# Layer 1's residual and softmax sums turned in 32x32 squares and carried through DRAM by GpSimd

## The chip, the cores and the metric

The kernel runs on one core of a Trainium2 chip. A core has a matrix engine (TensorE, PE in the views, with its weight loads as PEld), a vector engine (VectorE, DVE), a scalar engine (ScalarE, ACT), GpSimd (POOL) and a queue processor (SyncE, SP), which here issues all transfers. The engines run their own instruction streams in order and wait for each other by semaphores. The metric is the device time of one execution in microseconds; the time before is 1944.4 us, the median of three runs (1944.25 to 1944.41).

## The reference

Two layers of a decoder trunk on 1024 tokens of width 1024, all in float32. Layer 0 mixes tokens with gated linear attention in chunks, layer 1 with sparse attention: an indexer scores the keys of every query, the 256 best are kept, and 16 heads of 128 attend to these. Each layer then adds a residual, normalises, and adds a gated projection.

```python
def dsa_mixer(x, ...):                       # layer 1, shortened
    h = x @ w_in                             # q, k, v, z and the indexer's qi, ki, wi
    ...
    logits = jnp.where(valid, q_b . k_sel * ATTN_SCALE, -jnp.inf)
    probs = jax.nn.softmax(logits, axis=-1)
    o = probs . v_sel
    return (o * jax.nn.silu(z)) @ w_out

for i in range(DEPTH):
    y = gla_mixer(x, ...) if i % 3 == 0 else dsa_mixer(x, ...)
    x = layer_norm(ALPHA * x + y, ln_g[i], ln_b[i])          # the residual: ALPHA * x
    x = x + (p[i] @ ple_w[i]) * jax.nn.sigmoid(x @ ple_gate_w[i])
```

## The kernel before

Tokens are handled in two halves of 512, first both halves of layer 0, then both of layer 1. Activations lie feature-major: a tile [128, 512] has 128 features on the partitions and 512 tokens along them, and the 1024 features are 8 tiles k. For precision every matmul operand is split into a high part and the rest (`split`: ACT copies to the rounding type fp32r, DVE subtracts), and each product is three matmuls, high x high, high x low, low x high (`fm_block`: 24 matmuls of 128x512 for one block of 128 output features, into one of three PSUM banks `pb`). Weights are split on the way in during layer 0 and, by `split_ahead`, once more stored split in DRAM, from where later uses load them (`whi`, `wlo`).

The program is written by a planner in Python, `Flow`. It counts a planned time as it issues PE work (0.213 us for a 512-wide matmul, 0.109 for a transpose) and keeps a heap of functions with planned times (`fl.at`, `after`, `chain`); after every step of the PE stream it issues those that are due, so the place of an instruction in its engine's stream follows from its planned time. `feed_by` does the same for a generator at a fixed gap. A function may refuse and is tried again 0.3 us later.

In layer 1, a half is a row of slots, one for each head h from -1 to 15. In a slot PE runs the units of later or earlier work (q and z blocks for heads ahead, output products of heads done) while the attention of head h (PE: probabilities x V, tiles `ph`, `PT`, `o`) and the scores of head h + 1 (`A`: PE scores into `S`, DVE adds the mask and takes the extreme, ACT takes the exponential with its sum, DVE turns the result in 32x32 squares, SP stores it to DRAM and loads it back, which completes the transposition) are spread between them. `parts` then splits the loaded probabilities (ACT `ph`, DVE `PT`), `pv` multiplies them. The sum of each query's exponentials, `sm` [128 queries, 4], must become a row along the free axis: `inverse` takes the reciprocal, PE transposes it to [4, 128], ACT copies it out of PSUM, SP stores it as `row` and, in `to_all`, loads it to all partitions as `inv`; DVE multiplies z by it.

The layer's output is made token-major (`accumulate` adds a PSUM bank to `y[:, t, ...]`, 128 tokens by 512 features), since the norm runs over features. Its residual is layer 0's result x2, which lies feature-major in DRAM (`x2s`): `residual` loads each of the 8 tiles again, PE turns it with four transposes into a `pb` bank, and ACT writes it to y with the factor ALPHA. This happens at the ends of the slots of heads 0 to 3. `norm_steps` collects statistics and applies them in place; `tail` turns y back with 32 transposes and runs eight gate blocks (`("t", layer, b)`), whose operands `gx` come from splits. In half 0 of layer 1 a top-k search for the second half's queries runs in the background on DVE and ACT (`bg`).

Of the kernel before, what the change touches and what calls it, by code (L numbers as in the profile page):

```python
# [277 lines left out]
def trunk_kernel(ctx, tc, x_tok, x_T, p_T, pos, freq, g_q, g_k, g_v, g_z, g_a, g_a2, g_ba, g_gn, g_o,  # L278
# [178 lines left out]

    def narrow(w, n, t):
# [170 lines left out]
    def core_steps(u):  # L629
# [175 lines left out]
    def accumulate(parts, U, y, ch, rs=None, norm=None, ahead=1):  # L805
# [5 lines left out]
        for t, b in order:  # L811
# [11 lines left out]
            ys = y[:, t, ch * 512:ch * 512 + 512]  # L823
# [30 lines left out]
    def norm_steps(y, np_, eps, on_act=()):  # L854
# [6 lines left out]
        def norm(t, ch):  # L861
# [7 lines left out]
            dve.bn_stats(st8[:, t, ch], y[:, t, ch * 512:ch * 512 + 512])  # L869
# [5 lines left out]
            def apply():  # L875
                if t in on_act:
                    act.activation(y[:, t], y[:, t], AF.Identity, scale=rstd[:, t:t + 1], bias=mv[:, t, 1:2])
                else:
                    dve.tensor_scalar(y[:, t], y[:, t], mv[:, t, 0:1], rstd[:, t:t + 1],
                                      op0=OP.subtract, op1=OP.mult)  # L880
                f_done[t] = True
# [23 lines left out]
    def tail(layer, Pt, y, y_done, final, tp, xps, x_alloc, tmp, ple=(), first=None, shared=False, split_last=False):  # L905
# [10 lines left out]
        def xpose(k):  # L916
            fl.need(lambda: all(y_done))
            ps = xps()
            for t in range(4):
                fl.transpose(ps[:, t * 128:t * 128 + 128], y[:, t, k * 128:k * 128 + 128], ident)  # L920
# [20 lines left out]
        for b in range(NK):  # L941
            def ev(ps, ts=slice(0, HT), b=b):
# [3 lines left out]
                def gated():  # L946
# [3 lines left out]
                      (1.5, lambda: final(b, x1, ts) if cut else final(b, x1)))  # L950
            cut = split_last and b == NK - 1
            yield from fm_block(("t", layer, b), X, ev, *([(slice(0, 256), slice(256, HT))] if cut else []))
# [50 lines left out]
    def small_head(half, X, f32t, alloc, qalloc, tmp, spsum, kih, kil, res):  # L1003
# [30 lines left out]
        yield from fm_block(("ki",), X, ev_ki)  # L1034
        for b in range(4):
            def ev_qi(ps, b=b):
# [11 lines left out]
            yield from fm_block(("qi", b), X, ev_qi)  # L1048

    def small_kv(half, X, f32t, alloc, tmp, spsum, kh, kl, vh, vl, res):  # L1050
# [14 lines left out]
        def ev_v(ps):  # L1065
# [14 lines left out]
            chain((0, lambda: act.activation(vf, ps, AF.Copy, scale=0.5)), (1.2, turn))  # L1080
# [144 lines left out]
    def start_half(half):  # L1225
# [15 lines left out]
        def feed():  # L1241
            if half == 0:
                load(0, 1)
                W.loads(W.ns + 1)
                load(1, 1)
                W.loads(W.ns + 2)
                for k in range(2, NK, 2):
                    load(k, 2)
# [28 lines left out]
    for half in range(NH):  # L1277
        hs = slice(half * HT, half * HT + HT)
        if half == 0:
# [8 lines left out]
            feed_by(feeder, 0.0, 0.0)  # L1288
# [5 lines left out]
        y = X.y  # L1294

        def load_y(y=y, half=half):
# [50 lines left out]
        norm, y_done = norm_steps(y, lp, EPS / ALPHA ** 2)  # L1347
# [120 lines left out]
    def x2_tiles(half):  # L1468

        def load(k):  # L1470
            st = xp.tile([128, HT], F32, tag="xst", name="xst", bufs=2)
            nc.sync.dma_start(st, x2s[k, :, half * HT:(half + 1) * HT])
            return st
        st = load(0)
        for k in range(NK):
            nxt = load(k + 1) if k + 1 < NK else None
            yield
            yield k, st
            st = nxt

    def feed_x2(X, half):
        for i in range(2):
            nc.sync.dma_start(tabs[i], rope_s[i, 0:32, half * HT:(half + 1) * HT])
        for got in x2_tiles(half):
            if got:
                X.put(*got)
            yield

    def residual(st, y, half, ks, start, end):

        tiles = {}

        def load(k):
            tiles[k] = xp.tile([128, HT], F32, tag="xst", name="xst", bufs=2)
            nc.sync.dma_start(tiles[k], x2s[k, :, half * HT:(half + 1) * HT])

        def by_token(k):
            ps = pbank()
            for t in range(4):
# [253 lines left out]
    for half in range(NH):  # L1753
# [13 lines left out]
        for h, units in enumerate(plan, -1):  # L1767
# [36 lines left out]
            if h == 0:  # L1804
                y = xp.tile([128, 4, D], F32, tag="y", name="y")
# [87 lines left out]
```

## Time and profile before

| | |
|---|---|
| median of 3 runs | 1944.4 us |
| the profiled execution, its own time | 1945.97 us |
| its span, first to last instruction | 1944.2 us |
| granted TensorE clock | 1.000 |
| PE busy | 1924.8 us, 8912 matmuls and transposes |
| DVE, ACT, POOL busy | 1481.8, 1014.5, 55.2 us |
| bytes moved | 480.50 MB, all the kernel's own from one queue |

The page gives, for each engine, the busy time and its share of the span. Matmuls overlap in the pipeline, so that the durations of single ones add up to more than the busy time; what one costs PE is seen from start to start. The views named below are: the groups by line (an operation's count, busy time and mean duration, then the idle time before it and what ended that), the waits (who waited for whom: us in total, times, the longest), the timelines of an engine (start, duration), and the table of stretches.

### The profile page before, as it was taken

How to read it: one execution, taken by the hardware profiler on the slowest of the kernel's cores; microseconds unless marked ns; L12 is line 12 of the kernel's file. 1: busy time of each engine (PE TensorE's matmuls, PEld its weight loads, DVE VectorE, ACT ScalarE, POOL GpSimd, SP SyncE). 2: the span in 40 equal slices, each digit the busy share in tenths (PEclk: the TensorE clock that was granted, in tenths of full speed). 3: DMA queues.
4: the chain of work that ended last, by engine and by line, in shares of the span. 5: the costliest groups of instructions: out<-in, count | busy, mean ns of one | idle time of the engine just before them, and what ended most of it. 6: DMA issues, size and time to landing. Idle time of an engine off the chain costs nothing.

```text
span 1944.2 us, 26708 instructions
## 1 busy us (share of the span) xinstructions
PE 1924.8 (99%) x8912; PEld 1596.4 (82%) x8912; DVE 1481.8 (76%) x3039; ACT 1014.5 (52%) x1930; POOL 55.2 (3%) x115
## 2 busy tenths in 40 slices
PE   9999999999999999999999999999999999999999
PEld 7888888888788888888888888888878888888877
DVE  5777666696778888888859987778797887777873
ACT  5564636445564646464635676766443554434432
POOL 0000000010000000000100000000000000000000
PEclk9999999999999999999999999999999999999999
DMA  4567776767668777677686588877867998888873
GB/s 155 201 222 229 221 226 214 227 210 268 227 196 266 226 212 233 220 226 218 207 304 222 194 308 292 276 271 259 317 221 236 365 323 300 299 297 300 294 260 144
DMA packets 195818, 480.50 MB, mean 247 GB/s; under 512 B 22496, under 2 KB 39008, under 8 KB 189536
## 3 DMA queue, kind: packets, MB, share of 16 engines
q1 hardware_dynamic: 195680, 478.79, 73.8%
q8 instruction: 70, 1.15, 0.2%
q14 instruction: 68, 0.56, 0.1%
HBM read 338.98 MB, written 139.72 MB: 246 GB/s over the span
## 4 chain that ended last, share of the span: by engine, by line
PE 88%; DVE 4%; ACT 4%; DMA 2%; issue 1%; SPq 0%; POOL 0%; ACTq 0%; DVEq 0%
PE pb L58 66%; PE o L58 8%; PE U L58 6%; PE S L58 6%; DMA wlo<-wls 1%; PE tr L58 1%; ACT x L926 1%; DVE wlo L191 0%; DVE bn L869 0%; DMA xst<-x2s 0%; DMA y<-in_x_T 0%; DVE y L827 0%; PE pb L62 0%; PE ix L58 0%; DMA row<-uf 0%
## 5 line engine op out<-in xcount | busy, mean ns | idle before, releaser
L58 PE MATMUL pb<-x,whi 128*128 128x512 f32 x2272 | 705.4, 391 | 1.1 <-DVE x L411 1.0
L58 PEld LDWEIGHTS pb<-x,whi 128*128 128x128 f32 x2272 | 418.2, 188 | 81.2 <-DVE x L411 2.2
L58 PE MATMUL pb<-x,wlo 128*128 128x512 f32 x1136 | 442.8, 390 | 0.0
L58 PE MATMUL pb<-whi,u 128*128 128x512 f32 x1024 | 339.9, 392 | 1.5 <-ACT u L419 0.8
L58 PEld LDWEIGHTS pb<-x,wlo 128*128 128x128 f32 x1136 | 213.2, 188 | 45.7 <-DVE wlo L191 0.4
L58 PEld LDWEIGHTS pb<-whi,u 128*128 128x128 f32 x1024 | 192.1, 188 | 41.4 <-ACT u L419 1.2
L58 PE MATMUL pb<-wlo,u 128*128 128x512 f32 x512 | 199.8, 390 | 0.5 <-DMA wlo<-wls 0.5
L191 DVE TENSOR_TENSOR wlo<-wst,whi 128x512 fp32r<-128x512 f32 x232 | 154.3, 684 | 37.5 <-ACT whi L189 37.4
L189 ACT ACTIVATE whi<-wst 128x512 fp32r<-128x512 f32 x232 | 136.5, 622 | 69.4 <-DMA wst<-in_g_k 23.5
L1553 ACT ACTIVATE sq<-P,mx 128x128 f32<-128x128 f32 (+7 forms) x128 | 98.9, 773 | 88.2 <-DVE mx L1546 67.5
L58 PE MATMUL S<-kT,q 128*128 128x512 f32 (+2 forms) x576 | 122.4, 342 | 0.0
L1599 ACT ACTIVATE ph<-PT 128x512 fp32r<-128x512 f32 (+2 forms) x160 | 86.6, 559 | 65.6 <-PE o L58 46.3
L58 PEld LDWEIGHTS S<-kT,q 128*128 128x128 f32 x576 | 100.8, 188 | 18.1 <-DVE mx L1546 0.7
L58 PEld LDWEIGHTS pb<-wlo,u 128*128 128x128 f32 x512 | 96.2, 188 | 19.3 <-DMA wlo<-wls 1.3
L1597 DVE TENSOR_TENSOR PT<-PT,ph 128x512 fp32r<-128x512 f32 (+2 forms) x160 | 93.3, 594 | 21.1 <-ACT ph L1599 20.7
L1180 ACT ACTIVATE tk<-sc,tki 128x768 f16<-128x768 f32 (+2 forms) x90 | 92.8, 1031 | 18.3 <-DVE tki L1189 16.1
L1559 DVE STREAM_TRANSPOSE sq<-sq 128x128 f32<-128x128 f32 (+7 forms) x128 | 97.6, 768 | 3.2 <-ACT sq L1553 3.0
L237 DVE TENSOR_TENSOR pst<-pst,phi 128x512 fp32r<-128x512 f32 x130 | 88.7, 683 | 7.5 <-ACT phi L233 7.4
L736 ACT ACTIVATE junk<-o 128x512 bf16<-128x512 f32 x32 | 19.1, 597 | 142.1 <-DVE ot L731 109.8
L58 PE MATMUL o<-ph,vT 128*128 128x512 f32 (+2 forms) x320 | 92.4, 370 | 0.2 <-ACT ph L1599 0.2
L58 PE MATMUL pb<-whi,x 128*128 128x512 f32 x256 | 85.2, 391 | 0.7 <-ACT whi L189 0.7
L58 PE MATMUL U<-whi,x 128*128 128x512 f32 x256 | 84.5, 389 | 0.0
(324 smaller groups left out, 3325.0 us busy)
## 6 DMA issues: line engine op xcount, KB each, us to landing
whi<-whs SPq DMA_DIRECT2D x128, 512.0 KB
wlo<-wls SPq DMA_DIRECT2D x128, 512.0 KB
sqd<-sq SPq DMA_DIRECT2D x192, 256.0 KB
PT<-sqd SPq DMA_DIRECT2D x48, 1024.0 KB
whs<-phi SPq DMA_DIRECT2D x130, 256.0 KB
wls<-pst SPq DMA_DIRECT2D x130, 256.0 KB
wst<-in_g_z SPq DMA_DIRECT2D x32, 512.0 KB
wst<-in_g_o SPq DMA_DIRECT2D x32, 512.0 KB
```

What stands on the lines that cost most here:

```text
L58: self.pe.matmul(out, lhsT, rhs, start=start, stop=stop)
L189: self.nc.scalar.activation(hi[:, c], st[:, c], AF.Copy, scale=1.0 if gain is None else gain)
L191: self.nc.vector.tensor_sub(lo[:, c], st[:, c], hi[:, c].bitcast(F32))
L237: self.nc.vector.tensor_sub(st, st.bitcast(F32), hi.bitcast(F32))
L736: act.activation(junk, ps, AF.Square, accum_out=u["ss"][:, c:c + 1])
L926: act.activation(X1[k], ps, AF.Identity, scale=g, bias=b)
L1180: act.activation(junk()[:, :n], scs[j], AF.Sign, bias=cand[:, j:j + 1].bitcast(F32), accum_out=cnt[:, j:j + 1])
L1553: act.activation(to, rows, AF.Exp, scale=-1.0, bias=mx, accum_out=sm[:, t:t + 1])
L1559: dve.transpose(x, x)
L1597: dve.tensor_sub(lo, lo.bitcast(F32), hi.bitcast(F32))
L1599: chain((0, lambda: act.activation(hi, lo.bitcast(F32), AF.Copy)), (0.8, second))
```

## The change

In layer 1 the residual is no longer loaded again and turned by PE. The tile that the operands of a half were split from (`yt`: 8 feature-major tiles of x2) stays in place. For each k, `turn` lets DVE transpose the 32x32 squares of `y[:, k]` into an `xst` tile; `away` has GpSimd store it to DRAM in four DMAs of 32 partitions (tile `rd`); `back` has GpSimd load it over `y[:, k]`, now with tokens on the partitions. The eight blocks are planned 7.0 apart in half 0 and 10.5 apart in half 1. y so lies as `[p, k, a, t, i]`, features in runs of 32, and is reached through a function `y(t, a, n)`. The factor ALPHA is left out of the residual and its inverse goes into V's scale, with the norm's epsilon divided accordingly. The norm writes its result to x tiles (`to_rows`) and the tail reads it there. The next half's x2 is loaded after the norm, into the y tile, instead of through `xst` tiles.

The softmax sums become a row by squares as well: GpSimd clears a [128, 32] tile, DVE writes the reciprocals to 4 columns of it and transposes its squares, and GpSimd stores four pieces of 4 x 32. `inverse` is planned 8.5 (half 0) or 12 (half 1) after a slot's start; before, it was 3 ahead of the slot's end.

Three smaller edits go with it: `fm_two` runs two blocks together, the first k of both and then the last, for the first two gate blocks of each tail and for the indexer's ki and first qi; s3 of layer 0 ripens 2.2 after its operand's split, not 1.6; at the start x is fed with a gap of 1.3 planned us and two of its tiles are loaded ahead of the third weight.

```diff
+    def fm_two(keys, X, evacs, cut):
+        parts = [W.take(key) for key in keys]
+        banks = [pbank() for _ in keys]
+        for ks in (range(cut), range(cut, NK)):
+            for (hi, lo), ps, evac in zip(parts, banks, evacs):
+                for k in ks:
+                    xh, xl = X[k]
+                    at = slice(k * 128, k * 128 + 128)
+                    for i, (l, r) in enumerate(((hi, xh), (hi, xl), (lo, xh)), 3 * k):
+                        mm(ps, l[:, at], r, i == 0, i == 3 * NK - 1)
...
-                fl.ripe(st["At", c] + 1.6)
+                fl.ripe(st["At", c] + 2.2)
...
-                dve.tensor_add(ys, ps, ys)
+                dve.tensor_add(ys, ps.rearrange("p (x i) -> p x i", i=32), ys)
...
+                for there, row in to(t):
+                    if t in on_act:
+                        act.activation(there, row, AF.Identity, scale=rstd[:, t:t + 1], bias=mv[:, t, 1:2])
+                    else:
+                        dve.tensor_scalar(there, row, mv[:, t, 0:1], rstd[:, t:t + 1],
...
+        yield from fm_two([("t", layer, b) for b in range(2)], X, [gate(b, False) for b in range(2)], 4)
...
+        yield from fm_two([("ki",), ("qi", 0)], X, [ev_ki, query(0)], 5)
...
-            chain((0, lambda: act.activation(vf, ps, AF.Copy, scale=0.5)), (1.2, turn))
+            chain((0, lambda: act.activation(vf, ps, AF.Copy, scale=0.5 / ALPHA)), (1.2, turn))
...
-            feed_by(feeder, 0.0, 0.0)
+            feed_by(feeder, 0.0, 1.3)
...
+    def feed_x2(X, y_done, new_y):
...
+        while not all(y_done):
+            yield
+        y = new_y()
+        for k in range(NK + 3):
+            if k < NK:
+                nc.sync.dma_start(y[:, k], x2s[k, :, HT:2 * HT])
+            if k > 2:
+                X.put(k - 3, y[:, k - 3])
+            yield
...
-        def by_token(k):
-            ps = pbank()
-            for t in range(4):
-                fl.transpose(ps[:, t * 128:t * 128 + 128], tiles[k][:, t * 128:t * 128 + 128], ident)
-            act.activation(y[:, :, k * 128:k * 128 + 128], ps.rearrange("p (t c) -> p t c", c=128), AF.Copy,
-                           scale=ALPHA)
...
+        def turn(k):
+            sq = xp.tile([128, HT], F32, tag="xst", name="xst", bufs=2)
+            dve.transpose(sq.rearrange("p (m b i) -> p b m i", m=4, b=4), y[:, k])
+            after(1.0, lambda: away(k, sq))
+
+        def away(k, sq):
+            rd = dp.tile([4, 32, 4, 128], F32, tag="rd", name="rd", bufs=4)
+            for a in range(4):
+                pool.dma_start(rd[:, :, a].rearrange("m r x -> r m x"),
+                               sq[32 * a:32 * a + 32].rearrange("p (m x) -> p m x", m=4))
+            def back():
+                pool.dma_start(y[:, k], rd.rearrange("m r a x -> (m r) (a x)"))
+                st["y"] = st.get("y", 0) + 1
+            after(3.0, back)
+
         for k in range(NK):
+            fl.at(start + gap * k, lambda k=k: turn(k))
...
-            dve.reciprocal(st["sm", h], st["sm", h])
-            after(1.5, turn)
-        def turn():
-            ps = spsum()
-            fl.transpose(ps[0:4, 0:128], st["sm", h], ident)
-            inv = tmp1()[0:4, 0:128]
+            sums = l1.tile([128, 32], F32, tag="bn", name="sums")
+            pool.memset(sums, 0.0)
+            dve.reciprocal(sums[:, 0:4], st["sm", h])
+            dve.transpose(sums, sums)
             row = st["row", h] = dp.tile([4, 128], F32, tag="row", name="row", bufs=2)
             def out():
-                act.activation(inv, ps[0:4, 0:128], AF.Copy)
-                nc.sync.dma_start(row, inv)
+                for a in range(4):
+                    pool.dma_start(row[:, 32 * a:32 * a + 32], sums[32 * a:32 * a + 4])
...
-                fl.at(start + dur - 3.0, scale[0])
+                fl.at(start + (12.0 if half else 8.5), scale[0])
...
+                residual(st, yt, *((start + 5.0, 10.5) if half else (start + 33.0, 7.0)))
```

Three places show how instructions move. First PE, at the end of head 0's slot in half 0 of layer 1 (`pb<-x` is a q or z block, `o<-ph` and `o<-PT` are probabilities x V, `pb<-ident,xst` the residual's transposes, `S<-ident,sm` that of the sums), before:

```order
L62 MATMUL pb<-ident,xst 128x128 x4
L58 MATMUL o<-ph,vT_9843 128x512
L58 MATMUL o<-ph,vT_9844 128x512
L58 MATMUL o<-PT,vT_9843 128x512
L58 MATMUL pb<-x,whi 128x512 x2
L58 MATMUL pb<-x,wlo 128x512
L62 MATMUL pb<-ident,xst 128x128 x4
L58 MATMUL o<-ph,vT_9843 128x4x96
L58 MATMUL o<-ph,vT_9844 128x4x96
L58 MATMUL o<-PT,vT_9843 128x4x96
L62 MATMUL S<-ident,sm 4x128
```

and with the change:

```order
L58 MATMUL o<-ph,vT_9843 128x512
L58 MATMUL o<-ph,vT_9844 128x512
L58 MATMUL o<-PT,vT_9843 128x512
L58 MATMUL pb<-x,whi 128x512 x2
L58 MATMUL pb<-x,wlo 128x512
L58 MATMUL o<-ph,vT_9843 128x4x96
L58 MATMUL o<-ph,vT_9844 128x4x96
L58 MATMUL o<-PT,vT_9843 128x4x96
```

The transposes are gone and the products of the head stand in the same order.

Second GpSimd in the same slots, with the change (before, nothing stands there: the memset of `sq` ahead of the slots is followed by the norm's steps after them):

```order
L1629 MEMSET sums 128x32
L1636 DMA row<-sums 4x32 x4
L1521 DMA rd<-xst 32x4x128 x4
L1525 DMA y<-rd 128x512
L1521 DMA rd<-xst 32x4x128 x4
L1525 DMA y<-rd 128x512
L1629 MEMSET sums 128x32
L1636 DMA row<-sums 4x32 x4
```

Two blocks of the residual stand between the sums of one head and of the next, and each memset of `sums` comes behind a read-back.

Third DVE, in half 0 in head 0's slot, before (`PT` is the split of a part of the probabilities, `rt` and `qf` belong to a q block, `z<-z,inv` uses the sums of the head before):

```order
L1597 TENSOR_TENSOR PT<-PT,ph 128x4x96
L1159 TENSOR_SCALAR tkf<-tkf 128x1
L1597 TENSOR_TENSOR PT<-PT,ph 128x4x64
L1159 TENSOR_SCALAR tkf<-tkf 128x1
L999 TENSOR_TENSOR qf<-rt 32x512
L1605 RECIPROCAL sm<-sm 128x4
L1647 TENSOR_TENSOR z<-z,inv 128x512
```

and with the change:

```order
L1620 TENSOR_TENSOR PT<-PT,ph 128x4x96
L1186 TENSOR_SCALAR tkf<-tkf 128x1
L1630 RECIPROCAL sums<-sm 128x4
L1631 STREAM_TRANSPOSE sums<-sums 128x32
L1515 STREAM_TRANSPOSE xst<-y 128x4x4x32
L1620 TENSOR_TENSOR PT<-PT,ph 128x4x64
L1186 TENSOR_SCALAR tkf<-tkf 128x1
L1023 TENSOR_TENSOR qf<-rt 32x512
L1666 TENSOR_TENSOR z<-z,inv 128x512
```

The reciprocal, which now waits for the memset, and the two transposes stand ahead of a split of the probabilities.

More of the change, by code (lines that the diff above doesn't have):

```diff
@@ L822, in accumulate @@
                 continue
-            ys = y[:, t, ch * 512:ch * 512 + 512]
+            ys = y(t, ch * 512, 512)
             if rs is not None:
@@ L940, in tail, with gate, ev @@
             yield
-        for b in range(NK):
-            def ev(ps, ts=slice(0, HT), b=b):
+        def gate(b, cut):
+            def ev(ps, ts=slice(0, HT)):
                 sg = tmp()[:, ts]
@@ L950, in ev @@
                       (1.5, lambda: final(b, x1, ts) if cut else final(b, x1)))
+            return ev
+        yield from fm_two([("t", layer, b) for b in range(2)], X, [gate(b, False) for b in range(2)], 4)
+        for b in range(2, NK):
             cut = split_last and b == NK - 1
-            yield from fm_block(("t", layer, b), X, ev, *([(slice(0, 256), slice(256, HT))] if cut else []))
+            yield from fm_block(("t", layer, b), X, gate(b, cut),
+                                *([(slice(0, 256), slice(256, HT))] if cut else []))
     def rope_tables():
@@ L1032, in weights, with query, ev_qi @@
             res["w"] = wt
-        yield from fm_block(("ki",), X, ev_ki)
-        for b in range(4):
-            def ev_qi(ps, b=b):
+        def query(b):
+            def ev_qi(ps):
                 qf = f32t()
@@ L1047, in ev_qi @@
                 rope(qf, ci, si, swap_i, tmp, stack)
-            yield from fm_block(("qi", b), X, ev_qi)
+            return ev_qi
+        yield from fm_two([("ki",), ("qi", 0)], X, [ev_ki, query(0)], 5)
+        for b in range(1, 4):
+            yield from fm_block(("qi", b), X, query(b))
     def small_kv(half, X, f32t, alloc, tmp, spsum, kh, kl, vh, vl, res):
@@ L1245, in feed @@
                 load(1, 1)
+                load(2, 2)
                 W.loads(W.ns + 2)
-                for k in range(2, NK, 2):
-                    load(k, 2)
+                load(4, 2)
+                load(6, 2)
                 nc.sync.dma_start(ba, g_ba)
@@ L1466, in dz_phase @@
         yield from fm_block(("dz", h), X, ev)
[L1468 to L1474, printed above, removed]
-        for k in range(NK):
[L1476 to L1495, printed above, removed]
-        def by_token(k):
-            ps = pbank()
-            for t in range(4):
-                fl.transpose(ps[:, t * 128:t * 128 + 128], tiles[k][:, t * 128:t * 128 + 128], ident)
-            act.activation(y[:, :, k * 128:k * 128 + 128], ps.rearrange("p (t c) -> p t c", c=128), AF.Copy,
-                           scale=ALPHA)
-            st["y"] = k + 1
-        for i, k in enumerate(ks):
-            fl.at(start + 0.6 * i, lambda k=k: load(k))
-            fl.at(end - 3.6 + 1.6 * i, lambda k=k: by_token(k))
+    def feed_x2(X, y_done, new_y):
+        for i in range(2):
+            nc.sync.dma_start(tabs[i], rope_s[i, 0:32, HT:2 * HT])
+        while not all(y_done):
+            yield
+        y = new_y()
[4 more added lines that the diff above has]
+                X.put(k - 3, y[:, k - 3])
+            yield
```

50 lines of the change are left out of this document (31 added, 19 removed).

## The prediction

> **What bounds the kernel now.** I read the page first: the busy line, then its DMA queue.
>
> ```profile
> span 1944.2 us, 26708 instructions
> PE 1924.8 (99%) x8912; PEld 1596.4 (82%) x8912; DVE 1481.8 (76%) x3039; ACT 1014.5 (52%) x1930; POOL 55.2 (3%) x115
> q1 hardware_dynamic: 195680, 478.79, 73.8%
> ```
>
> PE is busy for all but 19.4 us of the span. One queue carries the kernel's own transfers, so no DMA of POOL's stands in this trace. The table of stretches, taken over three slots of layer 1's half 0 (where the first residual lies), shows how much room the others have (columns: stretch, its length, then busy time and count of PE, PEld, DVE, ACT, POOL, the granted clock, the DMA share, GB/s):
>
> ```profile
> 1118.00:1133.00 15.00, 14.82 (x74) 12.03 (x73) 12.85 (x34) 9.65 (x23) 0.00 (x0) 1.00 0.92 344
> 1133.00:1148.00 15.00, 15.00 (x77) 12.65 (x76) 12.51 (x34) 12.64 (x29) 0.00 (x0) 1.00 0.83 289
> 1148.00:1163.00 15.00, 14.14 (x72) 11.66 (x70) 13.05 (x37) 12.94 (x30) 0.00 (x0) 1.00 0.83 293
> ```
>
> PE sets the pace, DVE has 2.0 to 2.5 us free in 15, POOL does nothing. So PE instructions taken away count in full, if nothing else comes late.
>
> **What is removed.** The PE timeline at the first residual, where one group of four transposes and one transpose of softmax sums stand between matmuls:
>
> ```profile
> 1113.92 0.39 PE L58 MATMUL pb<-x,wlo 128*128 128x512 f32 x1
> 1114.15 0.60 PE L62 MATMUL pb<-ident,xst 128*128 128x128 f32 x4
> 1114.50 0.72 PE L58 MATMUL o<-ph,vT 128*128 128x512 f32 x2
> ...
> 1116.95 0.27 PE L62 MATMUL S<-ident,sm 128*4 128x128 f32 x1
> 1116.98 0.70 PE L58 MATMUL pb<-x,whi 128*128 128x512 f32 x2
> ```
>
> The durations overlap, so I cost from start to start: 1114.50 - 1114.15 = 0.35 us for four transposes and 0.03 for the sums. The 0.27 shown is pipeline length, not PE time. The counts, and what the evacuations cost ACT, come from the groups by line:
>
> ```profile
> L62 PE MATMUL pb<-ident,xst 128*128 128x128 f32 x64 | 9.6, 273 | 1.0 <-DMA xst<-x2s 1.0
> L62 PE MATMUL S<-ident,sm 128*4 128x128 f32 x32 | 8.7, 271 | 0.0
> L1501 ACT ACTIVATE y<-pb 128x512 f32<-128x512 f32 x16 | 9.5, 595 | 9.5 <-PE pb L62 9.0
> L1616 ACT ACTIVATE uf<-S 4x128 f32<-4x128 f32 x32 | 8.2, 255 | 21.1 <-PE S L62 21.0
> ```
>
> A: 64/4 = 16 groups x 0.35 = 5.6 us of PE. B: 32 x 0.03 = 1.0. C: the one wait of 1.0 us for `xst<-x2s`, since the tile turned is now already in SBUF. ACT loses 9.5 + 8.2 = 17.7 us, which is not on the path.
>
> **The smaller edits** aim at PE's own waits:
>
> ```profile
> PE pb L58 <- DVE wlo L191: 1.3, 3, 0.8
> PE pb L58 <- DVE gx L411: 0.8, 2, 0.6
> PE o L58 <- DVE Al L411: 0.7, 1, 0.7
> ```
>
> D: `fm_two` takes the first half of two blocks before the last operands are wanted, 12 matmuls later (12 x 0.227 = 2.7 us, three matmuls taking 0.68 in the timeline), against a longest wait of 0.6; and s3 ripens 0.6 later against 0.7. I take both waits in full: 1.5 (bounds 0 and 1.5). E: the start's waits of 1.3 are for low halves of weights that DVE reaches behind splits of x; with x fed every 1.3 planned us they alternate. I take 1.0 (bounds -0.7, if x then comes late, and 1.3). Gains: 5.6 + 1.0 + 1.0 + 1.5 + 1.0 = 10.1 us.
>
> **What is added.** DVE gets 16 transposes of 128x512 and 32 small transposes; the nearest rows:
>
> ```profile
> L731 DVE STREAM_TRANSPOSE ot<-o 128x512 f32<-128x512 f32 x29 | 20.8, 716 | 22.4 <-PE o L58 22.2
> L1605 DVE RECIPROCAL sm<-sm 128x4 f32<-128x4 f32 x32 | 5.4, 170 | 0.0
> ```
>
> A slot of half 0 gains 2 x 0.72 + 0.17 = 1.6 us of DVE work, under the 2.0 to 2.5 free, with little to spare: G = 0.5 us on PE for the lot (bounds 0 and 2.8: if only half of the 2 us lies where it is wanted, 0.6 to 0.7 in each of four slots). The normalised rows now go to x tiles, in two instructions of 512 where one of 1024 stood; four ple blocks of 6 matmuls (5.4 us) stand ahead of the first transpose that reads them: H = 0.2 (bounds 0 and 0.8). The next half's x2 loads move behind the norm, with the tail's 192 gate matmuls (43.6 us) over them, and cost nothing; uncovered, eight loads at one feed step of 2.3 each are 18 us. The wide add into y and the statistics keep their 512 elements, and the factor for the residual moves into the scale of an evacuation that is there anyway. SP loses 16 loads and 32 stores from its queue, which I count at nothing.
>
> **POOL's DMAs are the unknown.** Each block is four writes `rd<-xst` and one read `y<-rd`, each head four writes `row<-sums`. The nearest thing is the same pattern from SP in layer 0 (the view of tile od: shortest, median and longest issue in ns), and, in SP's timeline, how soon a stored row can be read on:
>
> ```profile
> L750 SPq DMA_DIRECT2D od<-ot x116: 303/434/1762, 87.2 to 917.9; - x116
> ```
>
> ```profile
> 1268.59 0.26 SPq L1617 DMA_DIRECT2D row<-uf  x1
> ...
> 1270.81 0.38 SPq L1625 DMA_DIRECT2D inv<-row  x1
> ```
>
> Let c be POOL's time for one DMA: 0.434 us if it is like SP's median, 1.762 if like SP's longest. The landing is 1270.81 - 1268.59 - 0.26 = 1.96 us. The read waits on POOL for its writes, and what queues behind it there is the next head's row and, above all, the memset of `sums`, for which DVE's reciprocal waits; behind the reciprocal on DVE stand the PT splits that PE multiplies next. How little lead these have, in the timelines of DVE and of PE:
>
> ```profile
> 1130.65 0.69 DVE L1597 TENSOR_TENSOR PT<-PT,ph 128x512 fp32r<-128x512 f32 x1 [0.74 <-ACT ph L1599]
> ...
> 1132.20 0.56 DVE L1597 TENSOR_TENSOR PT<-PT,ph 128x384 fp32r<-128x384 f32 x1
> ```
>
> ```profile
> 1131.40 0.50 PE L58 MATMUL o<-PT,vT 128*128 128x512 f32 x1
> 1133.22 0.34 PE L58 MATMUL o<-PT,vT 128*128 128x384 f32 x1
> ...
> 1147.20 0.40 PE L58 MATMUL o<-PT,vT 128*128 128x512 f32 x1
> ```
>
> Leads of 0.06 us (1130.65 + 0.69 to 1131.40) and 0.46. So a late POOL is a late DVE and nearly as late a PE. A slot is 1147.20 - 1131.40 = 15.8, less what A and B take out of it, 0.73: 15.1. Blocks stand 7.0 planned us apart, 7.46 real (0.227 us for a matmul planned at 0.213), two in a slot. POOL then needs 2 x (5c + 1.96) + 4c + 0.3 = 14c + 4.2, which fits while c is under 0.78. I take c = 0.7, a fifth of the way from SP's median of 116 to its single longest, the median being the row it is nearest to: 14.0 of 15.1, no lasting lateness. Still a read-back ends 5 x 0.7 + 1.96 = 5.5 us after its first write and is planned 3.2 after, so a memset close behind waits up to 2.3. Seven heads have one there; with 0 to 4 us between the two, the mean wait is 2.3 x 2.3 / 2 / 4 = 0.66, and after the leads PE sees some 0.3: F = 2.0 us (bounds 0, and 7 x 2.3 = 16 before any lasting lateness). Half 1, with 10.5 us between blocks, has room.
>
> [...]
>
> The sum: -10.1 + 2.0 + 0.5 + 0.2 = -7.4 us. The span goes from 1944.2 to 1936.8; the profiled execution's own time of 1945.97 lies 1.8 above its span, the median of the runs, 1944.4, only 0.2. **Forecast: 1937.0 us.**
>
> **Rivals.**
> 1. POOL cannot keep up in half 0. At c = 1.1, midway between the bounds, it needs 19.6 of 15.1, is 4.5 later after each slot, 18 after four, and PE waits it out at the reciprocals: -10.1 + 0.7 + 18 = +8.6, 1953.0. It decides from 14c + 4.2 = 15.1 + 9.4/4, c = 0.95. For it: POOL issues in order and waits for landings there at a DMA share of 0.83 to 0.92. Against it: SP's 434 ns for the same pattern.
> 2. Half 0 is paced by the softmax chain, not PE: at 1130.65 DVE had waited 0.74 for ACT's ph, and PE's next product waited for both. Then half 0's part is lost (8 x 0.35 + 16 x 0.03 = 3.3) and C with it: -3.1, 1941.3. Against it: ACT loses work ahead of that ph, and the second of the three stretches has PE busy throughout.
> 3. DVE holds POOL up. A DMA of POOL's that has to wait for the DVE instruction under way, a 0.72 us transpose or a PT split, has c near 0.7 + 0.7/2 = 1.05: POOL needs 18.9, 3.8 short, 15.2 over four slots, 1950.2. [...]
>
> **How the numbers follow.** Forecast 0.70, rival 1 0.14, rival 2 0.10, rival 3 0.06. The forecast's own range runs from 1931 (F, G and H at nothing, -10.1, and 3 us of the 19.4 idle gone with SP's shorter queue) to 1941. The whole goes up to 1947, where c is just under 1.0, leaving most of rivals 1 and 3 outside. This kernel's runs tell 0.2%, 3.9 us, from no change. Faster: nearly all of the forecast and a little of the rivals with c under 0.9, 0.69. Same: the forecast's edge, rival 2: 0.13. Slower: rivals 1 and 3 past 1948.3: 0.18.
>
> **What would show it.** Right: no `pb<-ident,xst` and `S<-ident,sm`, PE's busy time some 6 us lower, POOL's DMA rows near 0.7 us, little DVE waiting for POOL at the reciprocal, PE's gx and Al waits gone. Wrong: DVE idle at the reciprocal for microseconds (rivals 1 and 3: there the POOL rows are long, in 3 only beside DVE work), PE waiting for PT or ph in half 0 with POOL on time (rival 2), inv late for the z product, or new waits of PE in the first 50 us.

## The result, and the profile after

The changed kernel takes 1964.9 us (median of four runs, 1962.8 to 1975.5) where the kernel before, on the same chip, takes 1944.4: a ratio of 1.0111, interval 1.0089 to 1.0133. By the ratio it is slower by 21.6 us (20.5 by the medians) where 7.4 less had been forecast. The profiled execution is the longest of the four, so its waits are somewhat longer than the median's; prices below come from ratios of times, and the rows show places. A ratio's last digit, 0.0001, is 0.2 us.

From the page of the changed kernel, engines and the software DMA queue (which is POOL's: packets, MB, share of the time of 16 engines):

```profile
PE 1929.7 (98%) x8816; PEld 1597.9 (81%) x8816; DVE 1497.7 (76%) x3091; ACT 999.5 (51%) x1886; POOL 169.6 (9%) x355
...
q0 software_dynamic: 7424, 8.47, 1.4%
```

PE has the 96 fewer matmuls of the change (8912 before), yet more busy time (1924.8 before): part of it ran at a lower clock (granted 0.992 over the run, 1.000 before). The view of waits of the same kernel, for PE, DVE and POOL (us in total, times, longest):

```profile
PE o L58 <- DVE PT L1620: 23.4, 19, 5.8
PE S L58 <- DVE q L411: 3.0, 2, 2.5
PE o L58 <- ACT ph L1622: 2.8, 4, 1.6
```

```profile
DVE sums L1630 <- POOL sums L1629: 12.4, 6, 5.6
```

```profile
POOL sums L1629 <- DMA row<-sums: 71.9, 22, 5.7
...
POOL y L1525 <- DMA rd<-xst: 38.7, 7, 8.5
```

These are the rows that the prediction named as the sign of POOL being late. PE's waits for gx and Al are gone, and those for `wlo` in the start fell from 1.3 to 1.1. The view of tile rd gives POOL's own time for a DMA (ns, shortest, median, longest) and its time to landing:

```profile
L1521 POOL DMA_DIRECT2D rd<-xst x64: 548/551/683, 1097.3 to 1585.9; - x64
...
DMA to landing us min/median/max: 2.0/5.6/8.3
```

POOL is quicker at issuing than I had taken (0.55 us, not 0.7), and the landing is far longer (5.6 us, not 1.96). The timeline of one stall (start and length in us; in brackets the idle time before and what ended it):

```profile
1130.41 2.28 POOL L1521 DMA_DIRECT2D rd<-xst  x4
...
1137.22 0.57 POOL L1525 DMA_DIRECT2D y<-rd  x1 [4.53 <-DMA rd<-xst]
1137.78 0.14 POOL L1629 MEMSET sums<- 128x32 f32 x1
1137.95 0.18 DVE L1630 RECIPROCAL sums<-sm 128x4 f32<-128x4 f32 x1 [5.62 <-POOL sums L1629]
...
1138.30 0.65 DVE L1620 TENSOR_TENSOR PT<-PT,ph 128x512 fp32r<-128x512 f32 x1
...
1139.01 0.80 PE L58 MATMUL o<-PT,vT 128*128 128x512 f32 x1 [5.07 <-DVE PT L1620]
...
1139.60 1.06 PE L58 MATMUL pb<-x,whi 128*128 128x512 f32 x2
```

It reads downward as a chain: POOL's writes, their landing, the read-back, the memset behind it, DVE's reciprocal, the split of PT behind that, and PE. In the last row two matmuls take 1.06 us where they took 0.62 before the stall. The view by windows shows why, in its column PEclk, third from the end (before it busy time with instructions, PE's first, after it DMA share and GB/s). Its rows are three of the six stretches in which the clock was low; the last line adds up all six:

```profile
1122.27:1125.68 3.41, 3.41 (x12) 2.93 (x11) 3.00 (x10) 1.18 (x5) 0.00 (x0) 0.50 0.94 328
1135.92:1142.75 6.83, 3.74 (x10) 3.19 (x11) 4.17 (x12) 0.00 (x0) 4.47 (x9) 0.50 0.97 291
1173.47:1183.71 10.24, 5.92 (x16) 4.96 (x17) 2.37 (x6) 2.69 (x5) 2.79 (x6) 0.50 1.01 330
...
sum 30.74, PE 23.34 PEld 19.22 DVE 17.51 ACT 8.12 POOL 11.80; mean PE 3.89 PEld 3.20 DVE 2.92 ACT 1.35 POOL 1.97
```

With stalls of 5.1 us (from 1133.9) and 5.8 us (from 1172.0) PE was granted half its clock for 6.8 and 10.2 us. These stretches begin 2.0 and 1.5 us after the stall does, so that part of them passes while PE still waits; what they cost is half of the time in which PE had work, 3.74 and 5.92 us. In all six PE had work for 23.3 us, which is 11.7 us more than at full clock. The kernel before had no such stretch between the start and the end (granted clock 1.000).

### The profile page after: what moved, and what is told of

The parts are those of the page before. It is cut to its first block, busy times and chain, and to the rows that moved or that the text cites. A ratio compares the mean times of both kernels' runs of the same rounds, so it can differ in the third digit from the quotient of the medians.

```text
span 1973.8 us, 26916 instructions
## 1 busy us (share of the span) xinstructions
PE 1929.7 (98%) x8816; PEld 1597.9 (81%) x8816; DVE 1497.7 (76%) x3091; ACT 999.5 (51%) x1886; POOL 169.6 (9%) x355
## 4 chain that ended last, share of the span: by engine, by line
PE 83%; DVE 7%; DMA 5%; ACT 2%; issue 1%; POOL 1%; SPq 1%; DVEq 0%; POOLq 0%; ACTq 0%
PE pb L58 63%; PE o L58 7%; PE U L58 6%; PE S L58 5%; DMA rd<-xst 2%; DMA PT<-sqd 1%; DVE sq L1582 1%; PE tr L58 1%; DVE PT L1620 1%; ACT tk L1207 1%; SPq L1595 0%; DMA sqd<-sq 0%; DMA wst<-in_g_v 0%; DVE P L1569 0%; DVE tk L1230 0%
## 5 line engine op out<-in xcount | busy, mean ns | idle before, releaser
L58 PEld LDWEIGHTS pb<-x,whi 128*128 128x128 f32 x2272 | 422.6, 189 | 79.9 <-DVE x L411 1.8
L58 PEld LDWEIGHTS S<-kT,q 128*128 128x128 f32 x576 | 101.9, 191 | 23.3 <-DVE q L411 3.5
L1636 POOL DMA_DIRECT2D row<-sums x128 | 66.2, 523 | 459.7 <-DVE sums L1631 440.8
L58 PE MATMUL o<-PT,vT 128*128 128x512 f32 (+3 forms) x224 | 74.3, 355 | 23.5 <-DVE PT L1620 23.4
```

What stands on the lines that cost most here:

```text
L58: self.pe.matmul(out, lhsT, rhs, start=start, stop=stop)
L1636: pool.dma_start(row[:, 32 * a:32 * a + 32], sums[32 * a:32 * a + 4])
```

## The experiments

The theories, by the letters of the expectations: **P**, POOL's wait for landings holds DVE at the memset, DVE holds PE, and half clock follows. **C**, the added bytes crowd the DMA engines. **D**, **S** and **V**, DVE's added work or the sums' path. **W** and **Q**, PE's removed work is worth its time, or it is not, because operands set the pace. **O**, the order of matmuls. **H**, half clock after stalls.

### Taking POOL's wait away

The memset on DVE:

```
-            pool.memset(sums, 0.0)
+            dve.memset(sums, 0.0)
```

> The memset of sums is moved from POOL to DVE, so that DVE's reciprocal no longer waits for POOL; POOL still sits on each read-back until its writes have landed. Theory P (a late POOL holds DVE at the memset, DVE holds PE at PT, and PE then runs some microseconds at half clock): the four waits of 0.65 to 5.62 us of DVE for POOL in half 0 go (11.3 us), and with them PE's waits for PT there and most of the half-clock stretches of 3.4, 6.8 and 10.2 us (each costs PE half its length, 10.2 us in all): 1965 - 11 - 10 = 1944, at best 1940, at worst 1950. Theory C (the loss is the DMA engines' contention, which POOL's transfers add to): nothing of this depends on who clears sums, so 1963 to 1966. Theory D (DVE has become too full in half 0): DVE gets 32 memsets more, 1965 to 1968.

Measured 1960.6 us, 1.0083 (1.0065 to 1.0100). Only a quarter of the gain that P expected came. POOL stayed late, and DVE now met that lateness elsewhere; its waits between 1090 and 1210 us:

```profile
DVE sums L1629 <- DMA row<-sums: 3.0, 2, 1.6
DVE xst L1515 <- DMA rd<-xst: 2.7, 2, 1.4
```

The memset must wait until the row store that POOL issued late has read the tile, and the next block's transpose until POOL's writes have read theirs. A dependence through a buffer took the place of the one through the instruction.

The read-back later:

```
-            after(3.0, back)
+            after(9.0, back)
```

> The read-back of a residual block is planned 9.0 after its writes in place of 3.0; the memset stays on POOL. The writes took 2.0 to 8.3 us to land, median 5.6, so most read-backs should find their data there. Theory P: POOL's waits for rd<-xst (38.7 us before) fall under 10, DVE's waits for POOL sums from 12.4 to under 3, and the time to 1941 to 1950, much like the kernel with the memset on DVE. Theory C: the same bytes move at the same share, so 1963 to 1966; if the transfers only come into the way of others later, it could be 1970. Theory D: 1965 unchanged.

Measured 1955.6 us, 1.0050 (1.0034 to 1.0067): 12 us less than the change, and DVE's wait for POOL at the reciprocal is gone from the waits. P had expected more, 1941 to 1950, and POOL's waits for the writes' landings fell from 38.7 to 19.9 us, not under 10. Both edits together:

> Both edits together, memset on DVE and the read-back planned 9.0 after the writes. Theory P: no more than about 2 us better than the better of the two alone, since either takes away the same wait: 1939 to 1946. Theory C: 1963 to 1966. What is left above the 1937 of the forecast would be half 1's waits of PE for PT (8.8 us), where DVE had waited only 1.1 us for POOL: by P and C together some 1943 to 1947.

Measured 1955.0 us, 1.0049 (1.0034 to 1.0064), no better than the later read-back alone. P is shown and priced: the wait for landings in front of the memset costs 1.0111 - 1.0049 = 0.0062, **12 us**, the half clock behind its stalls included. It is not the whole, as P's 1939 to 1946 had it: 9.5 us above the kernel before are left.

### Whose landing it is

The four writes and the read-back of a block on SP in place of POOL:

```
-                pool.dma_start(rd[:, :, a]...
+                nc.sync.dma_start(rd[:, :, a]...
-                pool.dma_start(y[:, k], ...
+                nc.sync.dma_start(y[:, k], ...
-            after(3.0, back)
+            after(6.0, back)
```

> The residual's writes and read-backs are issued by SP in place of POOL, the read-back planned 6.0 after the writes; row stores stay with POOL and sums is still cleared there. It tells whether the late landing belongs to POOL's queue or to the load on the DMA engines. If to the queue, rd<-xst lands in about 2.8 us as SP's od<-ot does, in place of 5.6; if to the load, again in 4.5 to 6. Theory P: POOL has only row stores left, DVE's wait for POOL sums goes (under 1 us), and the time falls to 1940 to 1950, unless SP, waiting in its turn for a landing, delays sqd stores and PT loads: then PE waits for ph and PT in SP's name, and 1950 to 1965. Theory C: 1960 to 1966.

Measured 1958.4 us, 1.0067 (1.0052 to 1.0082). The view of tile rd:

```profile
L1521 SPq DMA_DIRECT2D rd<-xst x64: 303/447/1907, 1097.0 to 1576.5; - x64
...
DMA to landing us min/median/max: 1.7/5.6/9.0
```

The same median, 5.6 us, from the other queue: of the expectation's two alternatives it is the load, not POOL's queue. The DMA share here was 0.76 to 0.99 between 1100 and 1200 us; in the changed kernel SP's stores of the same 64 KB in layer 0 (`od<-ot`) landed in 2.8 us, at a mean share of 0.70 (87 to 918 us). SP could then not issue sqd stores while it waited (in half 1 ACT's `sq` waited 20.7 us behind `rd<-xst`), and PE waited for ph instead (4.2 us in half 1, longest 3.3).

### The change taken apart

The residual alone (sums as before the change), the sums alone, the small edits alone, and small edits with sums; each is a part of the diff shown above.

> The change without its softmax sums: the residual and the small edits as changed, the sums turned by PE, copied by ACT, stored by SP, as before the change. POOL's read-back keeps its early place, but nothing of DVE waits for POOL any more. Theory P (POOL at the memset) by what the three kernels before showed: worth about 10 us, so 1955, less what the sums cost DVE, plus 1 for their transposes on PE: 1953 to 1957. Theory C (the residual's way through DRAM, writes and reads of 4 MB each in place of reads of 4 MB, crowds sqd and PT while the DMA engines are busy at 0.9 and over): the rest of the loss stays whole, 1953 to 1957, with PE's waits for PT in half 1 at 6 us or more. Theory S (the rest comes from the sums' path, DVE's and the rows'): it goes, 1940 to 1946.

Measured 1954.0 us, 1.0044 (1.0029 to 1.0059), as P and C had it; S, by which it would have been 1940 to 1946, falls. POOL's read-back is early there, no memset stands behind it, and the time is that of the later read-back.

> The kernel before with the softmax sums alone done the new way (memset, reciprocal and small transpose, POOL's row stores), the residual still loaded and turned by PE. Theories P and C: POOL has only row stores of 0.5 KB, waits for their landing before the memset but for no read-back; DVE waits for POOL under 2 us; 1943 to 1946. Theory S: the loss that e3 still has, 10 us and over, stands here: 1952 to 1958. My forecast had 1.0 us of gain for it: 1943.5.

Measured 1943.5 us, 0.9991 (0.9982 to 1.0000), which is the forecast's 1.0 us of gain within the interval.

> The kernel before with the three small edits alone: two blocks side by side before the last operands, s3 ripe 0.6 later, and x fed every 1.3 in the start with its load order. My forecast counted 1.5 + 1.0 = 2.5 us for them: 1941.9. In the changed kernel PE's waits for gx (0.8) and Al (0.7) are gone and those for wlo fell only from 1.3 to 1.1, which gives 1.7: 1942.7. If their places were covered anyway: 1944.4.

Measured 1940.5 us, 0.9977 (0.9968 to 0.9987): 4.5 us of gain, more than the 2.5 forecast.

> The kernel before with the small edits and the softmax sums in squares, the residual loaded and turned by PE as before the change: the change less its residual. The two measured alone at 0.9977 and 0.9991 of the kernel before; if they add, 0.9968, 1939 against 1945. If the two get in each other's way (both use DVE in half 0), 1941 to 1944. This is the candidate that could beat both kernels, and the base of the next two runs.

Measured 1940.0 us, 0.9972 (0.9961 to 0.9982). Their gains add, and this kernel beats both. So the loss comes in with the residual: from 0.9972 to 1.0049 it costs 15 us even with POOL's waits out, although it takes 64 transposes off PE. The next runs take this 15 apart, on the kernel of 1940.0 as base.

On the kernel with both edits (1955.0) the transfers of half 1 were also moved ahead:

```
-                residual(st, yt, *((start + 5.0, 10.5) if half ...
+                residual(st, yt, *((start + 1.0, 4.5) if half ...
```

> The changed kernel with memset on DVE and the late read-back (measured 1955.0), and half 1's residual blocks at 1.0 + 4.5 per block in place of 5.0 + 10.5: they are done some 46 planned us sooner, about half of them before 1500 us, where the DMA engines were busy at 0.6 to 0.9 before the 0.98 of 1500 to 1580. Theory C: half 1's excess of about 15 us falls by a third to a half, 1947 to 1951. If it is the order of waits and not the load: 1955 as before, or worse, since POOL and DVE have 4.5 us for a block and its softmax row.

Measured 1959.4 us, 1.0071 (1.0058 to 1.0085), no gain, against C's 1947 to 1951: the other alternative, 1955 or worse. The blocks were then written between 1476 and 1518 us, and PE waited 3.6 us for one ph at 1509, which in the timeline ACT could not make before the load of PT had landed (DMA share 0.99 between 1500 and 1520 us). A lower DMA share some 20 us ahead (0.53 and 0.88 from 1460 to 1500 us in the kernel with both edits) was not room for them.

### Bytes and DVE's work, added without the rest

```
+                def more(k):
+                    rd = dp.tile([4, 32, 4, 128], F32, tag="rd", ...)
+                    for a in range(4):
+                        pool.dma_start(rd[:, :, a]..., kT[0][32 * a:32 * a + 32, 0:512]...)
```

> The kernel with small edits and sums (the run just before) and added DMA traffic alone: at the times of the residual's blocks POOL writes 4 x 64 KB of an SBUF tile to DRAM, which nobody reads. The residual in squares moves 8.5 MB by POOL in place of 4.3 MB of loads by SP, 4.2 MB more; these writes are 4.2 MB more too, but without DVE's transposes, and without a read-back. Theory C (bytes on DMA engines that are busy at 0.9 and over; 4.2 MB at the 345 GB/s that these stretches reach are 12 us): most of the loss comes back, 1939 + 8 to 15 = 1947 to 1954, with PE's waits for PT in half 1 at 4 us and over. Theory V (DVE's 16 transposes and what is queued behind them): 1939 to 1941.

Measured 1946.7 us, 1.0013 (1.0004 to 1.0023): 8 us for 4.2 MB. PE's waits there between 1090 and 1650 us:

```profile
PE pb L62 <- DMA xst<-x2s: 4.3, 2, 4.1
PE o L58 <- DVE PT L1623: 2.1, 3, 1.1
```

About half of it is a late load of the residual, a place that the changed kernel doesn't have: its longest wait, 4.1 us, was followed by 3.4 us of half clock besides (granted clock 0.93 between 1125 and 1150 us). Late PT is 2.1 us, 1.8 of them in half 1, so the bound of C (PT waits of 4 us there) was not met; the size of 8 us was. Where the bytes act is seen one step earlier, in ACT's waits for the load of the probabilities from 1090 to 1650 us, first of the base, then with the writes, last with DVE's added work alone (the next run):

```profile
ACT ph L1625 <- DMA PT<-sqd: 8.3, 4, 5.2
```

```profile
ACT ph L1625 <- DMA PT<-sqd: 20.2, 11, 5.4
```

```profile
ACT ph L1625 <- DMA PT<-sqd: 9.2, 7, 5.1
```

```
+                def more():
+                    dve.tensor_reduce(pad[:, 0:1], kT[0][:, 0:512].bitcast(F32), ...)
```

> The kernel with small edits and sums and added DVE work alone: at the times of the residual's transposes DVE makes one reduction over 128x512 f32 (about 0.6 us; the transpose took 0.71), 16 in all, with no DMA. Theory C: nothing beyond my forecast's 0.5 us for a fuller DVE, 1939 to 1941. Theory V: half 0 loses what e3 lost there beside POOL, some 10 us, 1945 to 1950.

Measured 1943.1 us, 0.9991 (0.9982 to 1.0000): 3.7 us for 16 instructions, between what C and V had expected. (The next expectation's 6.7 and 3.1 us are the same two costs by medians; 8.0 and 3.7 are by ratios.)

> The kernel with small edits and sums, and both additions at once: POOL's 64 writes of 64 KB and DVE's 16 reductions; PE still turns the residual. One by one they cost 6.7 and 3.1 us. If they add: 1950. If together they bring longer stalls and with these half clock: 1952 to 1957. If they share one slack: 1947.

Measured 1949.7 us, 1.0024 (1.0014 to 1.0033): 10.1 us above the base. They nearly add (8.0 + 3.7), and no half clock beyond one stretch of some 3.4 us came of it in the profiled execution, an estimate from its granted clock, 0.999 over the run.

### PE's transposes, taken away without the rest

The residual's rows are loaded straight into y, unturned:

```
-            tiles[k] = xp.tile([128, HT], F32, tag="xst", ...)
-            nc.sync.dma_start(tiles[k], x2s[k, ...])
+            nc.sync.dma_start(y...[:, k * HT:(k + 1) * HT], x2s[k, ...])
...
-            ps = pbank()
-            for t in range(4):
-                fl.transpose(ps[...], tiles[k][...], ident)
-            act.activation(y[...], ps..., AF.Copy, scale=ALPHA)
```

> The kernel with small edits and sums, and its residual neither turned nor scaled: x2's rows are loaded straight into y, at the same times and in runs of the same 2 KB, so PE's 64 transposes and ACT's 16 evacuations are left out (the residual then stands in the wrong order and without its factor). Measures the forecast's largest gain alone: 16 x 0.35 = 5.6 us and 2.6 us of PE's waits for xst. Theory W (PE's work is worth its time): 1940 - 5.6 - 2 = 1932 to 1935. Theory Q (softmax chain, DVE and DMA pace the first four heads, PE just meets them): 1937 to 1940.

Measured 1943.1 us, 0.9986 (0.9977 to 0.9995): not 5.6 to 8 us faster than its base of 0.9972 but, if anything, 2.7 slower (the intervals overlap). PE's waits from 1090 to 1650 us, first of the base, then without transposes:

```profile
PE pb L62 <- ACT tk L1205: 1.2, 1, 1.2
PE pb L62 <- DMA xst<-x2s: 1.1, 1, 1.1
...
PE o L58 <- DVE PT L1623: 0.3, 1, 0.3
```

```profile
PE o L58 <- DVE PT L1618: 6.2, 9, 1.3
PE S L58 <- DVE q L411: 2.1, 1, 2.1
```

With less work on PE the same operands are late: PT by 6.2 us where it was 0.3, q by 2.1. The timelines show the second, of the base and without transposes:

```profile
1115.59 0.63 PE L58 MATMUL pb<-x,whi 128*128 128x512 f32 x2
1116.06 0.39 PE L58 MATMUL pb<-x,wlo 128*128 128x512 f32 x1
1116.29 0.63 PE L58 MATMUL pb<-x,whi 128*128 128x512 f32 x2
1116.75 0.39 PE L58 MATMUL pb<-x,wlo 128*128 128x512 f32 x1
1116.98 0.54 PE L58 MATMUL S<-kT,q 128*128 128x256 f32 x3
```

```profile
1113.99 0.63 PE L58 MATMUL pb<-x,whi 128*128 128x512 f32 x2
1114.46 0.39 PE L58 MATMUL pb<-x,wlo 128*128 128x512 f32 x1
1114.68 0.40 PE L58 MATMUL S<-kT,q 128*128 128x256 f32 x2
1117.21 0.73 PE L58 MATMUL S<-kT,q 128*128 128x256 f32 x4 [2.13 <-DVE q L411]
```

S stands one projection group sooner: the plan's clock counts PE's work, so that leaving out 0.44 planned us per block moves what is planned by time ahead of matmuls, to a place where q is not ready. The order printed ahead of the prediction ended before this row; the changed kernel's S has such a wait too (2.5 us, above).

To tell the order from the work, the plan's time was kept:

```
         def by_token(k):
+            fl.now += 4 * 0.109
             st["y"] = k + 1
```

> The kernel with the unturned residual (no PE transposes, no factor, rows in the wrong order), whose plan counts 0.436 us for each block's four transposes although they are not there, so that every engine keeps the order of the kernel with transposes. Theory O (the order moved matmuls ahead of their operands): PE's 2.1 us wait for q goes, the half clock behind it too, and of the 5.6 us most comes back, 1934 to 1937. Theory Q (the operands' chain sets the pace): PE waits for PT as before, 1939 to 1943.

Measured 1937.9 us, 0.9965 (0.9952 to 0.9977), about 4 us better than without it, and 1.4 better than the base, where the intervals overlap. PE's waits from 1090 to 1650 us:

```profile
PE o L58 <- DVE PT L1619: 3.7, 4, 2.7
PE o L58 <- ACT ph L1621: 1.5, 2, 0.9
```

The wait for q is gone, and in half 1 the waits for PT, 3.6 us without it, fell to 0.3: O. But 5.2 us of waits for PT and ph came in its place, nearly all in half 0, the longest of 2.7 us, and with them some 3.4 us of half clock, an estimate from the granted clock over the run (0.999, in the base 1.000): Q. The time lies between what O and Q had expected. Of PE's 5.6 us at most a few come back, and only with the order kept.

All three together, without the chain of write, landing and read-back:

> As the run just before, and the residual unturned besides (loaded straight into y, no PE transposes, no evacuation, no factor): all that the squares remove and add, in work and bytes, without the chain of write, landing and read-back. Theory W: what the two additions gave less 5.6 to 8, 1942 to 1945 if they gave 1950. Theory Q: as without the removal, 1950 and over; then the removal is worth nothing where the other two are, and the loss of 1955 is explained but for some 5 us. If it reaches 1955, explained whole.

Measured 1953.1 us, 1.0037 (1.0023 to 1.0051). Over the run without transposes (0.9986) the bytes and DVE's work again cost 9.9 us, and over the run with them (1.0024) the removal again gives nothing. Its waits from 1090 to 1650 us, shown first, resemble those of the change with POOL's waits out:

```profile
PE o L58 <- DVE PT L1618: 10.8, 15, 1.3
PE S L58 <- DVE q L411: 2.5, 1, 2.5
```

```profile
PE o L58 <- DVE PT L1620: 7.9, 10, 2.0
PE S L58 <- DVE q L411: 3.0, 2, 2.5
PE o L58 <- ACT ph L1622: 1.7, 3, 0.7
```

From 1.0037 to 1.0049 only 2.3 us are left, within the intervals, for the read-back's dependence and for what else the two kernels differ in (the norm's x tiles, the moved loads of x2, y's order, the memset's engine).

The planned time kept in the changed kernel without POOL's waits, by the same line at the sixteen places where the transposes stood:

> The changed kernel with memset on DVE and the late read-back (measured 1955.0), and the same 0.436 us counted where the 16 blocks' transposes stood. Theory O: the 2.5 us wait for q and its half clock go, some 5 us or more in all, 1947 to 1950; still above the kernel before by the writes and read-backs (6.7) and DVE's transposes (3.1). Theory Q: 1953 to 1956.

Measured 1951.4 us, 1.0040 (1.0025 to 1.0056), against 1.0049 without: better by less than the intervals tell, between O's 1950 and Q's 1953, and still slower than before. Waits for q fell from 3.0 to 1.0 us, and those for ph rose from 1.7 to 4.3.

A last try on the kernel of 1940.0: the residual's loads sooner, `start + 0.1` in place of `start + 1.3`.

> The kernel with small edits and sums, and the residual's loads planned 1.2 sooner in each of the four heads (0.1 after the slot's start in place of 1.3). PE waits there for xst 1.3 us twice in half 0 (one row for DMA, one for ACT's clearing of the tile). If the load's own start decides: 1 to 2 us less, 1938 to 1939. If the tile comes free too late anyway, or the load then stands before a store that is more urgent: 1940 to 1941.

Measured 1940.7 us, 0.9975 (0.9966 to 0.9984): no difference.

### Stalls and the clock

```
+                    if half and g == 1:
+                        for _ in range({1: 1, 3: 2, 5: 3, 7: 4, 9: 6, 11: 8, 13: 10}.get(h, 0)):
+                            dve.tensor_reduce(pad[:, 0:1], bias_t[7], ...)
```

> The kernel before with added work alone: ahead of the split of one PT group in heads 1, 3, 5, 7, 9, 11 and 13 of half 1, DVE takes 1, 2, 3, 4, 6, 8 and 10 extra reductions over one bias tile. It makes stalls of PE of growing length in a stretch that had none, to see what length is followed by granted clock at half. Theory H (a stall is paid again by half clock; in the changed kernel 1.4 us brought 3.4 us of it, 2.7 brought 3.4, 5.2 brought 6.8, 6.0 brought 10.2): every stall from about 1.4 us on is followed by 3.4 us or more at half clock, the longest by 6.8 to 10.2. Rival (the half clock belonged to that run or to POOL's DMAs): full clock throughout, and the time grows only by the stalls.

One run, 1984.2 us. PE's waits in four stretches (around 1676, 1732, 1790 and 1851 us), and windows of the granted clock in the same stretches, with full clock between the first two:

```profile
PE o L58 <- DVE PT L1600: 3.4, 1, 3.4
PE o L58 <- DVE PT L1600: 3.8, 1, 3.8
PE o L58 <- DVE PT L1600: 8.1, 1, 8.1
PE o L58 <- DVE PT L1600: 10.1, 1, 10.1
```

```profile
1681.20:1684.60 3.40, 3.40 (x9) 2.64 (x8) 3.13 (x7) 1.37 (x3) 0.00 (x0) 0.50 0.83 184
1685.00:1735.00 50.00, 47.75 (x226) 39.69 (x224) 40.24 (x78) 18.70 (x36) 0.00 (x0) 1.00 0.82 290
1735.80:1742.60 6.80, 6.08 (x14) 4.79 (x15) 6.04 (x11) 1.15 (x2) 0.00 (x0) 0.50 0.50 120
...
1793.80:1804.00 10.20, 5.01 (x12) 3.95 (x13) 9.37 (x12) 1.64 (x3) 0.00 (x0) 0.50 0.29 65
...
1855.40:1865.40 10.00, 3.84 (x9) 3.04 (x10) 9.86 (x12) 1.15 (x2) 0.00 (x0) 0.50 0.12 27
```

H holds in a kernel without any of the change: stalls of 3.4, 3.8, 8.1 and 10.1 us brought 3.4, 6.8, 10.2 and at least 10.0 us of half clock, and between them it was full (1.00 from 1685 to 1735, 1743 to 1793 and 1804 to 1855 us). The price did not grow with the length: behind the first stall PE had work through all 3.40 us, in the windows of the two longest for only 5.01 and 3.84 us, since there the half clock began while PE still waited. The smallest additions made waits of 0.7 us at most, after which the clock stayed full (1.00 from 1500 to 1660 us), so the range between was not reached here.

## Why the prediction was wrong

The forecast was -7.4 us, the result +21.6. The runs give this account, each item a difference of two ratios: small edits and sums -5.4; PE's transposes gone +2.5 to 2.7 (within the intervals); the residual's bytes and DVE's turns +10; write, landing and read-back in order +2.3 (within the intervals); POOL's waits in front of the memset +12. The sum is 21.6 by construction, since each kernel follows on the one before it; the items of -5.4, 10 and 12 are those clear of noise.

- **Gain A failed, as a step.** The prediction priced 16 x 0.35 us of PE work as 5.6 us of time, since PE showed as busy throughout. Leaving just this work out cost 2.7 us where 5.6 of gain were forecast, and with the order kept it gave 1.4. That PE was busy for 99% of the span did not mean that its operands were early: the prediction's own leads, 0.06 and 0.46 us, were the room that it had, and 0.35 us taken out twice in a slot is more than that. The prediction used these leads for POOL's lateness (F) and not for its own gain. Rival 2 is this mechanism, for half 0 and at a price of 4.3 us, and in half 0 the waits stay when the order is kept. Half 1's waits for PT (3.6 us) went when the order was kept (0.3), so there it was the plan's moved order, which no term had.
- **Gain B and D + E held in their sign.** The sums gave 1.8 us (0 to 3.5) against a forecast net of about 1; the small edits 4.5 (2.5 to 6.2) against 2.5, whose bounds end at 2.8. PE's waits for wlo, gx and Al, on which D and E rest, sum to 2.8 before, and the start's own fell by only 0.2, so about 2 us of the gain is not explained by these terms.
- **Cost F failed, by its landing.** The formula has two landings in a slot's need: 14c + 2 x landing + 0.3. With c = 0.7 and 1.96 it is 14.0 of 15.1; with the measured 0.55 and 5.6 it is 19.2. That is rival 1's outcome by the term that rival 1 did not vary. No run shows a c of just under 1.0, at which the upper end of the whole range, 1947, was put: POOL's c measured 0.55. The 1.96 came from one store of 2 KB, in a row at 1268 us; the residual's writes are 64 KB each, at a DMA share of 0.75 to 0.95 between 1120 and 1180 us. F was 2.0 us (bounds 0 and 16); it measured 12. Half 1 had room, as forecast: DVE waited 1.1 us for POOL there.
- **Half clock was in no term.** Every stall was priced at its length. In the profiled executions half clock took 11.7 us in the changed kernel and about 6.7 with POOL's waits out, stretches in which PE still waited included (an estimate from granted clocks of 0.94 and 0.93 in 1100 to 1125 and 1175 to 1200 us, 0.94 and 0.89 in 1500 to 1520 and 1520 to 1540); both are contained in the items above.
- **G was mis-sized**, 0.5 (bounds 0 and 2.8) against 3.7 us for 16 reductions of 0.67, which stood in for the transposes.
- **The bytes were counted at nothing.** "SP loses 16 loads and 32 stores from its queue, which I count at nothing" overlooks that POOL's 8.5 MB replace 4.3 MB on engines that were at a share of 0.98 between 1500 and 1580. 4.2 MB more cost 8 us where they were added alone, and ACT's waits for the probabilities rose from 8.3 to 20.2 us.
- **Rival 3 fell**: the residual's writes took POOL 548 to 683 ns each, beside any DVE work, where it had 1.05 us.

What stays open: why the half-1 transfers did not profit from an earlier place, what H and the moved loads of x2 cost by themselves (they lie in the 2.3 us), and how the 10 us divide in the changed kernel itself, since half of the added writes' cost entered through a load that it doesn't make.

## What to carry to other kernels

Work taken off the busiest engine was worth time only as far as its operands were ready early enough at that place (5.6 us of PE's work gave 1.4 at best); read their lead in the timeline before the work is priced, and after such an edit compare the order, because a plan that counts that engine's time moves everything behind it. A landing time is to be taken from transfers of the same size in the same stretch of DMA share (a 2 KB store gave 1.96 us, the 64 KB writes took 5.6), and an engine that waits for one in the order of its stream should have nothing urgent behind it (the memset behind POOL's waits cost 12 us). A gain that is doubtful in one part is found by building the parts alone: here the parts without the residual beat both kernels, 1940.0 us.

## What the runs showed of the hardware

PE's granted clock fell to half with short stalls. In the changed kernel the stalls of 2.5, 5.1 and 5.8 us (from 1119.2, 1133.9 and 1172.0 us) were followed by 3.4, 6.8 and 10.2 us at 0.50, beginning 3.0, 2.0 and 1.5 us after the stall's start. Of the shorter ones those of 2.0 us (from 1530.8, with one of 1.1 close by) and 1.6 us (from 1889.8) brought 3.4 us each, and one of 1.3 us (from 1196.8) brought none; one of 1.2 us brought 3.4 us (from 1494.3) with another of 0.5 close by, and the rest, of 1.0 us and less, brought none. In the kernel before, the longest between 1090 and 1930 us was 1.0 us, and the clock stayed full. In the run with the memset on DVE two matmuls right after a stall of 3.3 us (from 1164.1) still took 0.62 us, as ahead of it. So in these kernels, which keep PE full, a stall of 3.4 us cost about 5.1, an estimate from the first window of the run with added stalls.
